# A diffusion layer's prologue: x by token halves, with squares, sums, power, rows and the first products by halves

## The chip, the cores and the metric

The kernel runs on one core of a Trainium2 chip. The core has a matrix engine (TensorE, PE in the profile, with its weight loads listed apart as PEld), three engines for elementwise work (VectorE or DVE, ScalarE or ACT, GpSimd or POOL), an engine that mainly issues transfers (SyncE or SP), and 16 DMA engines that carry the transfers between HBM and the on-chip memory SBUF. TensorE writes into PSUM, an accumulation memory of eight banks. The metric is the time of one execution on the device in microseconds (us), and the median over runs is compared.

## The reference

One layer over 512 latent tokens and 256 context tokens, each 1024 wide, in fp32. Only the start of it is touched by the change:

```python
def _rmsnorm(x, gain):
    xf = x.astype(jnp.float32)
    y = xf * lax.rsqrt(jnp.mean(xf * xf, axis=-1, keepdims=True) + EPS)
    return y.astype(x.dtype) * gain

def _modulate(x, gain, shift, scale):
    return _rmsnorm(x, gain) * (1 + scale) + shift

mod = jax.nn.silu(c) @ w_ada[l] + b_ada[l]
mod_c = jax.nn.silu(c_ctx) @ w_ada[l] + b_ada[l]
sh1, sc1, g1, sh2, sc2, g2 = jnp.split(mod[:, None, :], 6, axis=-1)
csh1, csc1, cg1, csh2, csc2, cg2 = jnp.split(mod_c, 6)
a_lat = _modulate(x, norm_mix[l], sh1, sc1)
a_ctx = _modulate(xc, norm_mix[l], csh1, csc1)
p_lat = jnp.split(a_lat @ w_in, split_at, axis=-1)
```

So for each token the squares of its 1024 values are summed and turned into a reciprocal root; x is multiplied by it and by a scale per channel, a shift per channel is added, and the result goes into the input projection. Scale and shift come from a product of silu(c) with a weight matrix of 1024 x 6144. Behind it follow pooling branches, a bidirectional mLSTM, an output projection, a second norm, a SwiGLU FFN and a final norm, which the change leaves as they are.

## The kernel before

Activations lie transposed: channels on the 128 partitions, tokens along the row. The 1024 channels are eight tiles of 128, numbered k, and x is eight tiles of 128x512. fp32 products are made of two rounded parts, high and low, of both operands: three matmuls (high by high, high by low, low by high) stand for one. A tile `a` of the modulated input therefore has a high part (ScalarE, line 300) and a low part (VectorE, line 303), and a weight block has `wh` (ScalarE, line 339) and `wl` (VectorE, line 341).

The prologue goes like this. `parm` (norm gains, biases, c) is fetched first on SP's queue (line 104), then x in four transfers of 512 KB (line 132), the identity matrix (line 137), and then, in turns, modulation weights `ada` of 1 MB for a tile k (line 275) and the first input-projection weights `wr` of 384 KB (line 338). `keep_warm` (line 143) issues filler matmuls of a zeroed 128x128 tile, whose result nobody reads; `WARM` (line 46) holds five counts of them.

ScalarE squares seven of the eight x tiles (line 355), VectorE squares the eighth (line 358) and adds them up into two tiles (lines 357, 359). TensorE sums these two over the partitions with the square tile as the stationary operand and two columns of ones as the moving one: four token blocks of 128, two tiles, so eight matmuls (line 362). `power` brings the sums to the power of -0.5 (VectorE line 243, GpSimd line 245), and `rstd_rows` spreads the result over the partitions with four matmuls against the identity (line 253).

`mod_rows(k)` multiplies silu(c) by the modulation weights with eight matmuls on quarter columns of the array (line 279), and ScalarE copies the 128x256 result (line 282). `mod_cols(k)` turns it by two transposes (line 288); VectorE adds the four quarters (line 290) and makes shift and scale (lines 292, 293). `stage(k)` fetches the weights, and makes `wh`, `wl` and the two parts of the tile `a` (lines 339, 299, 300, 341, 303). `products(k, lo, hi, parts)` then adds tile k into the six accumulators of 128x512 of the first six column blocks (line 347). In the steady state one step of the loop over k has 18 product matmuls, one `mod_rows`, one `mod_cols` and one `stage`, two tiles ahead. At k = 4 the context's column sums (line 237) and at k = 5 its rows (line 253) come in.

The order of the work around the change is written by hand: inside the manual schedule TensorE, ScalarE and VectorE run their instructions in the order of the code, and each engine waits in that order for its operands. SP issues its transfers in order too; a tile's buffer must be free before the transfer into it is issued (three buffers for `ada`, three for `wr`, two for `wh` and `wl`).

Of the kernel before, what the change touches and what calls it, by code (L numbers as in the profile page):

```python
# [10 lines left out]
F32 = mybir.dt.float32  # L11
F32R = mybir.dt.float32r
AF = mybir.ActivationFunctionType
ALU = mybir.AluOpType
# [3 lines left out]
P = 128  # L18
D = 1024
KT = D // P  # L20
T = 512
TC = 256
# [10 lines left out]
LINE = 256  # L33
HALFLINE = 64
NEXT = 48
WMAX = KT // 2 * (DH + NG)
# [14 lines left out]
def layer_kernel(ctx: ExitStack, tc, xT, cT, w0, w1, wv0, wv, wada_a, wada_b, par, crow, bg, wpool,  # L51
                 wout, wffi, wffo, icnt, consts, out):
    nc = tc.nc
    V = nc.vector
# [30 lines left out]
    open_pool("main", ("wr", "wh", "wl", "tmp", "small", "rc", "rc2"))  # L85
# [5 lines left out]
    def small(shape, nm, dtype=F32, home="small"):  # L91
        return homes[home].tile(shape, dtype, name=nm, tag=nm, bufs=1)
# [20 lines left out]
    warm = small([P, P], "warm", home="x")  # L113
# [6 lines left out]
    bsc1 = small([P, KT], "bsc1")  # L120
# [5 lines left out]
    quarter_mg = small([P, KT], "quarter_mg")  # L126
    V.tensor_scalar(quarter_mg, parm[:, C_MG:C_MG + KT], 0.25, None, ALU.mult)

    x_sb = []
    for k in range(0, KT, 2):  # L130
        xx = tl("x", [P, 2 * T], F32, KT // 2)
        nc.sync.dma_start(xx, xT[:, k * T:(k + 2) * T])
        x_sb += [xx[:, :T], xx[:, T:]]
    ones = small([P, P], "ones")
    nc.gpsimd.memset(ones, 1.0)
    ident = small([P, P], "ident")
    nc.sync.dma_start(ident, consts[:, :P])

    wbank = PS("pat")

    def keep_warm(n, zero):
        for i in range(n):
            nc.tensor.matmul(wbank[:, :zero.shape[-1]], zero, zero, start=True, stop=True)
# [60 lines left out]
    class SumSq:  # L204


        q = None
# [48 lines left out]
        free = False  # L256
        banks = []

    ALL = slice(0, T)
    HALF = (slice(0, T // 2), slice(T // 2, T))  # L260
# [11 lines left out]
    def mod_rows(k):  # L272

        raw = tl("ada", [P, KT, 256], F32, 3)
        nc.sync.dma_start(raw.rearrange("p k c -> p (k c)"), wada_a[k])
        acc = PS()
        for r in range(2):
            for g in range(4):
                nc.tensor.matmul(acc[32 * g:32 * g + 32, :256], sil[:, 4 * r + g, :], raw[:, 4 * r + g, :],
                                 start=r == 0, stop=r == 1, tile_position=(0, 32 * g))  # L280
        rows = S("tmp")
        nc.scalar.copy(rows[:, :256], acc[:, :256])
        return rows

    def mod_cols(k, rows):
        bank = PS()
        for w in range(2):
            nc.tensor.transpose(bank[:, w * P:(w + 1) * P], rows[:, w * P:(w + 1) * P], ident)
        both = tl("rc2", [P, 2, 2], F32, 2)
        V.tensor_reduce(both, bank[:, :2 * P].rearrange("p (w g j) -> p w j g", w=2, g=4)[:, :, 0:2, :],  # L290
                        mybir.AxisListType.X, ALU.add)
        V.tensor_scalar(shm[:, k, :], both[:, 0, :], pcol(C_BA, k), None, ALU.add)
        V.tensor_scalar(sm[:, k, :], both[:, 1, :], bsc1[:, k:k + 1], pcol(C_NM, k), ALU.add, ALU.mult)

    def modulate(src, r, scale, shift, h, l, between=None):

# [9 lines left out]
    aT, acT = [], []  # L306
# [3 lines left out]
    stc = SumSq()  # L310
# [21 lines left out]
    w_first = []  # L332
# [11 lines left out]
    def products(k, lo, hi, parts=((0, 0), (0, 1), (1, 0))):  # L344
        for i in range(lo, hi):
            for w, x in parts:
                nc.tensor.matmul(acc0[i], w_first[k][i][w], aT[k][x], start=k + w + x == 0, stop=k == KT - 1 and w == 1)  # L347

    nf = len(FIRST)


    bank = PS()
    sq = [S("tmp") for _ in range(KT)]
    for k in range(KT - 1):
        nc.scalar.activation(sq[k], x_sb[k], AF.Square)
        if 0 < k < KT - 2:
            V.tensor_add(sq[0], sq[0], sq[k])
    V.tensor_mul(sq[KT - 1], x_sb[KT - 1], x_sb[KT - 1])
    V.tensor_add(sq[KT - 1], sq[KT - 2], sq[KT - 1])
    for t, q in enumerate((sq[0], sq[KT - 1])):  # L360
        for i in range(T // P):
            nc.tensor.matmul(bank[:, 2 * i:2 * i + 2], q[:, i * P:(i + 1) * P], ones[:, 0:2], start=t + i == 0,
                             stop=t == 1, skip_group_check=True)
        if t == 0:
            keep_warm(WARM[1], warm)
    sd = stx.power(bank, T // P)
    rows = mod_rows(0)
    keep_warm(WARM[2], warm)
    mod_cols(0, rows)
    r = stx.rstd_rows(sd, ALL)  # L370
    stage(0, r)
    keep_warm(WARM[3], warm)
    rows = mod_rows(1)
    keep_warm(WARM[4], warm)
    products(0, 0, nf, ((0, 0),))
    mod_cols(1, rows)
    nc.scalar.copy(rs_x, r)
    stage(1, rs_x)
    for k in range(KT):
        parts = ((0, 0), (0, 1), (1, 0))[0 if k else 1:]  # L380
        products(k, 0, nf // 2, parts)
        if k + 2 < KT:
            rows = mod_rows(k + 2)
        products(k, nf // 2, nf, parts)
        if k + 2 < KT:
            mod_cols(k + 2, rows)
            stage(k + 2, rs_x)
        if k < 4:
            nc.sync.dma_start(cxt[k], cT[:, k * 512:(k + 1) * 512])
            for e in range(2):  # L390
                stc.add(c_sb[2 * k + e], slice(0, TC))
# [620 lines left out]
    parts = {}  # L1012
# [397 lines left out]
```

## Time and profile before

| | us |
|---|---|
| median of 3 runs | 885.37 (885.31 to 886.13) |
| the profiled execution's own time | 886.11 |
| its span in the profile | 884.3 |
| TensorE busy in the span | 874.4 (99%) |
| VectorE, ScalarE, GpSimd busy | 614.7, 436.7, 66.7 |
| start of the first product matmul (line 347) | 18.12 |
| granted TensorE clock | 0.998 |

The span is the time from the first to the last instruction in the profile; the execution's own time is 1.8 us longer. The profile's chain of waits follows the work that ended last back through what released each piece; its first column is the start in us, the second the duration, then the engine, the tile and the line, and xN counts the hardware's instructions that are merged in the row. One fp32 matmul of a 128-column stationary tile shows as two such instructions: the 32 filler matmuls of the start stand as x64. Matmul ends are modelled, so starts are the safer numbers.

### The profile page before, as it was taken

To read this page: it belongs to the slowest core of one execution; us is meant where nothing else is said; L and a number is where in the kernel's file an instruction comes from. 1 tells how busy PE (TensorE), PEld (TensorE's weight loads), DVE (VectorE), ACT (ScalarE), POOL (GpSimd) and SP (SyncE) were. 2 spreads that over 40 slices of the span, in tenths; PEclk is the share of its full clock that TensorE was granted. 3 is DMA by queue.
4 is the path that set the end of the run, shared out by engine and by line. 5 is a ranking of instruction groups with operands and counts; after the bars stand their busy time and mean duration, and the time that the engine had idled before them with its cause. 6 is when DMAs were issued, how large, how long until landed. Compare 5 with 4: busy or idle time off the path is not lost.

```text
span 884.3 us, 15057 instructions
## 1 busy us (share of the span) xinstructions
PE 874.4 (99%) x5920; PEld 797.7 (90%) x5920; DVE 614.7 (70%) x1187; ACT 436.7 (49%) x823; POOL 66.7 (8%) x93
## 2 busy tenths in 40 slices
PE   9999999999999999999999999999999999999997
PEld 7689798899888998889988899999889998899996
DVE  4678677877876787767886767795366753867644
ACT  4464354455344453444455446673255741666542
POOL 0000010020000100000000000120011100111000
PEclk9999999999999999999999999999999999999999
DMA  9863021436252542434454830384366643755502
GB/s 349 324 196 113 25 72 57 164 113 180 72 187 88 170 141 84 155 109 135 142 149 125 294 111 1 104 221 107 95 176 147 145 119 87 206 142 125 144 1 96
DMA packets 41446, 120.88 MB, mean 137 GB/s; under 512 B 4480, under 2 KB 8864, under 8 KB 40352
## 3 DMA queue, kind: packets, MB, share of 16 engines
q1 hardware_dynamic: 35904, 109.96, 38.2%
q0 software_dynamic: 5472, 9.96, 6.8%
q8 instruction: 46, 0.75, 0.3%
q14 instruction: 24, 0.20, 0.1%
HBM read 116.22 MB, written 3.69 MB: 136 GB/s over the span
## 4 chain that ended last, share of the span: by engine, by line
PE 96%; DVE 1%; ACT 1%; DMA 1%; issue 0%; DVEq 0%; SPq 0%; ACTq 0%
PE ps L187 14%; PE ps L189 13%; PE ps L188 13%; PE ps L197 8%; PE ps L195 8%; PE ps L194 8%; PE pat L347 3%; PE ps L578 3%; PE ps L579 3%; PE ps L580 3%; PE pat L187 2%; PE pat L189 2%; PE pat L188 2%; PE pat L792 2%; PE pat L793 2%; PE pat L794 2%
## 5 line engine op out<-in xcount | busy, mean ns | idle before, releaser
L157 ACT CAST wh<-wr 128x1024 fp32r<-128x1024 f32 (+3 forms) x78 | 78.9, 1011 | 102.7 <-PE ps L188 45.6
L158 DVE TENSOR_TENSOR wl<-wr,wh 128x1024 fp32r<-128x1024 f32 (+3 forms) x78 | 92.6, 1188 | 35.9 <-ACT wh L157 23.8
L194 PE MATMUL ps<-a,wh 128*128 128x512 f32 x272 | 106.5, 392 | 0.0
L195 PE MATMUL ps<-a,wh 128*128 128x512 f32 x272 | 106.3, 391 | 0.0
L187 PE MATMUL ps<-act,wh 128*128 128x512 f32 (+1 forms) x199 | 69.2, 348 | 0.0
L188 PE MATMUL ps<-act,wh 128*128 128x512 f32 (+1 forms) x199 | 69.0, 347 | 0.0
L189 PE MATMUL ps<-act,wl 128*128 128x512 f32 (+1 forms) x199 | 69.0, 347 | 0.0
L197 PE MATMUL ps<-a,wl 128*128 128x512 f32 x272 | 68.0, 390 | 0.0
L195 PEld LDWEIGHTS ps<-a,wh 128*128 128x128 f32 x272 | 51.1, 188 | 10.2
L194 PEld LDWEIGHTS ps<-a,wh 128*128 128x128 f32 x272 | 51.1, 188 | 10.2
L197 PEld LDWEIGHTS ps<-a,wl 128*128 128x128 f32 x272 | 50.8, 188 | 10.5
L1030 POOL DMA_DIRECT2D ol<-in_wffi x38 | 33.4, 897 | 254.7 <-ACT ol L1029 124.4
L187 PE MATMUL ps<-hp,gh 128*128 128x256 f32 x176 | 49.9, 284 | 0.4 <-ACT gh L176 0.4
L189 PE MATMUL ps<-hp,ol 128*128 128x256 f32 x176 | 48.8, 277 | 0.5 <-DVE ol L1027 0.5
L188 PE MATMUL ps<-hp,gh 128*128 128x256 f32 x176 | 49.0, 278 | 0.0
L1251 DVE SCALAR_TENSOR_TENSOR x<-ps,lb,x 128x512 f32<-128x512 f32 (+1 forms) x32 | 19.6, 616 | 42.1 <-PE ps L189 42.1
L189 PE MATMUL ps<-hp,gl 128*128 128x256 f32 x176 | 48.9, 278 | 0.0
L187 PE MATMUL ps<-hp,oh 128*128 128x256 f32 x176 | 48.8, 277 | 0.0
L188 PE MATMUL ps<-hp,oh 128*128 128x256 f32 x176 | 48.7, 277 | 0.0
L537 DVE SCALAR_TENSOR_TENSOR pb<-pb,crow_s 128x1024 f32<-128x1024 f32 x32 | 38.9, 1233 | 10.1 <-DMA pb<-in_wada_b 10.1
L187 PEld LDWEIGHTS ps<-act,wh 128*128 128x128 f32 x199 | 37.5, 188 | 4.8
L188 PEld LDWEIGHTS ps<-act,wh 128*128 128x128 f32 x199 | 37.5, 188 | 4.8
(365 smaller groups left out, 2726.4 us busy)
## 6 DMA issues: line engine op xcount, KB each, us to landing
wr<-in_w SPq DMA_DIRECT2D x42, 512.0 KB, 3.5
pb<-in_wada_b SPq DMA_DIRECT2D x32, 512.0 KB, 4.2
wr<-in_wffi SPq DMA_DIRECT2D x25, 512.0 KB, 4.3
ur<-in_wffi SPq DMA_DIRECT2D x19, 512.0 KB, 4.0
ol<-in_wffi POOLq DMA_DIRECT2D x38, 256.0 KB, 4.9
ada<-in_wada_a SPq DMA_DIRECT2D x8, 1024.0 KB, 9.8
wr<-in_wffo SPq DMA_DIRECT2D x16, 448.0 KB, 3.6
wr<-in_wout SPq DMA_DIRECT2D x8, 512.0 KB, 3.5
```

What stands on the lines that cost most here:

```text
L157: nc.scalar.copy(wh, raw[:, :n])
L158: V.tensor_sub(wl, raw[:, :n], wh.bitcast(F32))
L187: nc.tensor.matmul(dst, wh, ah, start=first and i == 0, stop=False, skip_group_check=on)
L188: nc.tensor.matmul(dst, wh, al, start=False, stop=False, skip_group_check=on)
L189: nc.tensor.matmul(dst, wl, ah, start=False, stop=last and i == n - 1, skip_group_check=on)
L194: nc.tensor.matmul(dst, wh, ah, start=first and i == 0, stop=False)
L195: nc.tensor.matmul(dst, wh, al, start=False, stop=False)
L197: nc.tensor.matmul(dst, wl, ah, start=False, stop=last and i == len(wparts) - 1)
L347: nc.tensor.matmul(acc0[i], w_first[k][i][w], aT[k][x], start=k + w + x == 0, stop=k == KT - 1 and w == 1)
L537: V.scalar_tensor_tensor(wa[:, :D], wa[:, :D], 0.5, crow_s, ALU.mult, ALU.mult, accum_out=mods[:, i:i + 1])
L578: nc.tensor.matmul(acc[:, :n], ah, wh, start=kk == 0, stop=False)
L1030: nc.gpsimd.dma_start(l, dram, accum_op=ALU.add)
```

## The change

The change is confined to the prologue. It does seven things.

- The transfers: `parm` and the first token halves of x tiles 4 to 7 are issued on ScalarE's queue, the first halves of tiles 0 to 3 on SP's. x arrives in eight transfers of 256 KB (a pair of tiles by 256 tokens, rows of 1 KB). On SP's queue the identity, the first modulation weights (in two transfers of 512 KB) and then the four second halves follow.
- The squares: for each half, and each pair of tiles, one square tile is made (ScalarE for pairs 0 and 2, VectorE for pair 1, both for pair 3). They are no longer added on VectorE: TensorE sums each of them over the partitions, four matmuls for a pair, 16 for a half, 32 in all.
- Power and rows run by halves, on two token blocks each; the first half's rows stand in the middle of `mod_rows(0)`.
- `mod_cols` has two ordinary matmuls against a 128x2 tile `pick` instead of two transposes and VectorE's reduction, for all eight k. The result has two columns per matmul.
- The first tile's 18 products are done by halves: 36 matmuls with 256 moving columns.
- `mod_rows(2)` stands behind all products of k = 0, and `mod_cols(2)` and `stage(2)` in the middle of k = 1.
- The filler counts: 18 at the start, and 2, 0, 2, 4 behind the pairs of the first half, 2 inside `mod_rows(0)`, 4 behind it, and 2, 0, 2, 2 behind the pairs of the second half; 38 before and 38 now.

```diff
-WARM = (32, 2, 2, 2, 0)
+WARM = (18, (2, 0, 2, 4), 2, 4, (2, 0, 2, 2))
-    nc.sync.dma_start(parm, par)
+    nc.scalar.dma_start(parm, par)
-    x_sb = []
-    for k in range(0, KT, 2):
-        xx = tl("x", [P, 2 * T], F32, KT // 2)
-        nc.sync.dma_start(xx, xT[:, k * T:(k + 2) * T])
-        x_sb += [xx[:, :T], xx[:, T:]]
+    def x_load(queue, j, c):
+        queue.dma_start(halves(pair[j])[:, :, c], halves(xT[:, 2 * j * T:(2 * j + 2) * T])[:, :, c])
+    for j in range(KT // 2):
+        x_load(nc.scalar if j >= KT // 4 else nc.sync, j, HALF[0])
...
     nc.sync.dma_start(ident, consts[:, :P])
+    ada0 = tl("ada", [P, KT, 256], F32, 3)
+    for r in range(2):
+        nc.sync.dma_start(ada0[:, 4 * r:4 * r + 4, :].rearrange("p k c -> p (k c)"),
+                          wada_a[0][:, 4 * r * 256:(4 * r + 4) * 256])
+    for j in range(KT // 2):
+        x_load(nc.sync, j, HALF[1])
...
     def mod_cols(k, rows):
         bank = PS()
-        for w in range(2):
-            nc.tensor.transpose(bank[:, w * P:(w + 1) * P], rows[:, w * P:(w + 1) * P], ident)
-        both = tl("rc2", [P, 2, 2], F32, 2)
-        V.tensor_reduce(both, bank[:, :2 * P].rearrange("p (w g j) -> p w j g", w=2, g=4)[:, :, 0:2, :],
-                        mybir.AxisListType.X, ALU.add)
+        for w in (1, 0):
+            nc.tensor.matmul(bank[:, 2 * w:2 * w + 2], rows[:, w * P:(w + 1) * P], pick, start=True, stop=True)
...
-    for t, q in enumerate((sq[0], sq[KT - 1])):
-        for i in range(T // P):
-            nc.tensor.matmul(bank[:, 2 * i:2 * i + 2], q[:, i * P:(i + 1) * P], ones[:, 0:2], start=t + i == 0,
-                             stop=t == 1, skip_group_check=True)
+    def column_sums(h, j, sq):
+        for e in range(2):
+            for i in range(2):
+                nc.tensor.matmul(sums[h][:, 2 * i:2 * i + 2], sq[:, (2 * e + i) * P:(2 * e + i + 1) * P], ones[:, 0:2],
+                                 start=j + e + i == 0, stop=j + e == KT // 2, skip_group_check=True)
...
+    for j in range(KT // 2):
+        sq = squares(0, j)
+        column_sums(0, j, sq)
+        keep_warm(WARM[1][j], warm)
+    sd = stx.power(sums[0], 2)
...
+    rows = mod_rows(0, lambda: (rs.append(rows_of(sd)), keep_warm(WARM[2], warm)))
+    keep_warm(WARM[3], warm)
+    sq2 = [squares(1, j) for j in range(2)]
     mod_cols(0, rows)
...
+    sq2 += [squares(1, j) for j in range(2, KT // 2)]
+    for j in range(KT // 2):
+        column_sums(1, j, sq2[j])
+        keep_warm(WARM[4][j], warm)
+    sd = stx.power(sums[1], 2)
...
+    products(0, 0, nf, ((0, 0),), HALF[0])
+    rs.append(rows_of(sd))
...
+    products(0, 0, nf, ((0, 1),), HALF[0])
+    products(0, 0, nf, ((1, 0),), HALF[0])
+    rows = mod_rows(1)
+    products(0, 0, nf, ((0, 0),), HALF[1])
+    products(0, 0, nf // 2, ((0, 1),), HALF[1])
     mod_cols(1, rows)
...
```

What stands on an engine's queue is shown by its own list of instructions (the names are tiles with a running number; x4 counts equal rows). TensorE before, from its start to the first product of k = 0; line 143 is the filler, 362 the column sums, 279 `mod_rows`, 288 `mod_cols`, 253 the rows, 347 a product:

```order
L143 MATMUL pat_109<-warm 128x128 x32
L362 MATMUL ps_158<-ones,tmp_159 128x2 x4
L143 MATMUL pat_109<-warm 128x128 x2
L362 MATMUL ps_158<-ones,tmp_166 128x2 x4
L279 MATMUL ps_196<-ada_194,sil 32x256 x8
L143 MATMUL pat_109<-warm 128x128 x2
L288 MATMUL ps_209<-ident,tmp_205 128x128 x2
L253 MATMUL ps_216<-ident,rc_191 128x128 x4
L143 MATMUL pat_109<-warm 128x128 x2
L279 MATMUL ps_237<-ada_235,sil 32x256 x8
L347 MATMUL ps_148<-a_226,wh_222 128x512
```

Eight column sums stand ahead of the first product, and both `mod_rows(0)` and `mod_rows(1)`.

TensorE of the changed kernel, the first part of the same stretch; line 157 is now the filler, 383 the column sums, 295 `mod_rows`, 389 the rows:

```order
L157 MATMUL pat_116<-warm 128x128 x18
L383 MATMUL pat_146<-ones,tmp_152 128x2 x4
L157 MATMUL pat_116<-warm 128x128 x2
L383 MATMUL pat_146<-ones,tmp_160 128x2 x4
L383 MATMUL pat_146<-ones,tmp_166 128x2 x4
L157 MATMUL pat_116<-warm 128x128 x2
L383 MATMUL pat_146<-ones,tmp_174 128x2 x4
L157 MATMUL pat_116<-warm 128x128 x4
L295 MATMUL ps_189<-ada_109,sil 32x256 x4
L389 MATMUL ps_194<-ident,rc_185 128x128 x2
L157 MATMUL pat_116<-warm 128x128 x2
L295 MATMUL ps_189<-ada_109,sil 32x256 x4
```

The first half's 16 column sums stand ahead of `mod_rows(0)`, which is cut in two by the rows of that half. The rest of the stretch follows at once; line 304 is the new `mod_cols`, 360 a product:

```order
L157 MATMUL pat_116<-warm 128x128 x4
L304 MATMUL ps_213<-pick,tmp_203 128x2 x2
L383 MATMUL pat_145<-ones,tmp_209 128x2 x4
L157 MATMUL pat_116<-warm 128x128 x2
L383 MATMUL pat_145<-ones,tmp_211 128x2 x4
L383 MATMUL pat_145<-ones,tmp_226 128x2 x4
L157 MATMUL pat_116<-warm 128x128 x2
L383 MATMUL pat_145<-ones,tmp_228 128x2 x4
L157 MATMUL pat_116<-warm 128x128 x2
L360 MATMUL ps_142<-a_223,wh_219 128x256
```

The second half's 16 column sums stand ahead of the first product, and `mod_rows(1)` has moved behind the first half's 18 products.

More of the change, by code (lines that the diff above doesn't have):

```diff
@@ L270, in layer_kernel, with mod_rows @@
     shm = small([P, KT, 2], "shm")
-    def mod_rows(k):
-        raw = tl("ada", [P, KT, 256], F32, 3)
-        nc.sync.dma_start(raw.rearrange("p k c -> p (k c)"), wada_a[k])
+    pick = small([P, 2], "pick")
+    def mod_rows(k, between=None):
+        if k == 0:
+            raw = ada0
+        else:
+            raw = tl("ada", [P, KT, 256], F32, 3)
+            nc.sync.dma_start(raw.rearrange("p k c -> p (k c)"), wada_a[k])
         acc = PS()
         for r in range(2):
+            if r and between:
+                between()
             for g in range(4):
@@ L342, in stage, with products @@
         w_first.append([(wh[:, i * P:(i + 1) * P], wl[:, i * P:(i + 1) * P]) for i in range(len(FIRST))])
-    def products(k, lo, hi, parts=((0, 0), (0, 1), (1, 0))):
+    def products(k, lo, hi, parts=((0, 0), (0, 1), (1, 0)), c=ALL):
         for i in range(lo, hi):
             for w, x in parts:
-                nc.tensor.matmul(acc0[i], w_first[k][i][w], aT[k][x], start=k + w + x == 0, stop=k == KT - 1 and w == 1)
+                nc.tensor.matmul(acc0[i][:, c], w_first[k][i][w], aT[k][x][:, c],
+                                 start=k + w + x + c.start == 0, stop=k == KT - 1 and w == 1, skip_group_check=True)
@@ L366, in layer_kernel, with squares @@
-    sd = stx.power(bank, T // P)
-    rows = mod_rows(0)
-    keep_warm(WARM[2], warm)
-    mod_cols(0, rows)
-    r = stx.rstd_rows(sd, ALL)
-    stage(0, r)
-    keep_warm(WARM[3], warm)
+    sums = [acc0[4 - h] for h in range(2)]
+    def squares(h, j):
+        sq = S("tmp")
+        src, dst = halves(pair[j])[:, :, HALF[h]], halves(sq)
+        if j == KT // 2 - 1:
+            nc.scalar.activation(dst[:, 0], src[:, 0], AF.Square)
+            V.tensor_mul(dst[:, 1], src[:, 1], src[:, 1])
+        elif j % 2:
+            V.tensor_mul(dst, src, src)
+        else:
+            nc.scalar.activation(dst, src, AF.Square)
+        return sq
@@ new lines, in column_sums, with rows_of @@
+    def column_sums(h, j, sq):
[3 more added lines that the diff above has]
+                                 start=j + e + i == 0, stop=j + e == KT // 2, skip_group_check=True)
+    def rows_of(sd):
+        r = PS()
+        for i in range(2):
+            nc.tensor.matmul(r[:, i * P:(i + 1) * P], sd[:, i:i + 1].broadcast_to([P, P]), ident, start=True, stop=True)
+        return r[:, :T // 2]
@@ new lines, in layer_kernel @@
+    nc.sync.dma_start(raw[:, :n], w0[0])
+    t0, a0h, a0l = S("tmp"), S("a", F32R), S("a", F32R)
+    aT.append((a0h, a0l))
+    w_first.append([(wh[:, i * P:(i + 1) * P], wl[:, i * P:(i + 1) * P]) for i in range(nf)])
+    V.scalar_tensor_tensor(t0[:, HALF[0]], x_sb[0][:, HALF[0]], sm[:, 0, 0:1], rs[0], ALU.mult, ALU.mult)
+    sq2 += [squares(1, j) for j in range(2, KT // 2)]
[3 more added lines that the diff above has]
+    sd = stx.power(sums[1], 2)
@@ new lines, in layer_kernel @@
+    nc.scalar.activation(a0h[:, HALF[0]], t0[:, HALF[0]], AF.Identity, bias=shm[:, 0, 0:1])
+    V.scalar_tensor_tensor(a0l[:, HALF[0]], t0[:, HALF[0]], shm[:, 0, 0:1], a0h[:, HALF[0]].bitcast(F32),
+                           ALU.add, ALU.subtract)
+    for c in (slice(0, n // 2), slice(n // 2, n)):
+        nc.scalar.copy(wh[:, c], raw[:, c])
+        V.tensor_sub(wl[:, c], raw[:, c], wh[:, c].bitcast(F32))
+    nc.scalar.copy(rs_x[:, HALF[0]], rs[0])
+    products(0, 0, nf, ((0, 0),), HALF[0])
@@ L373, in layer_kernel, with context_squares @@
     rows = mod_rows(1)
-    keep_warm(WARM[4], warm)
-    products(0, 0, nf, ((0, 0),))
+    products(0, 0, nf, ((0, 0),), HALF[1])
+    products(0, 0, nf // 2, ((0, 1),), HALF[1])
     mod_cols(1, rows)
-    nc.scalar.copy(rs_x, r)
     stage(1, rs_x)
-    for k in range(KT):
-        parts = ((0, 0), (0, 1), (1, 0))[0 if k else 1:]
-        products(k, 0, nf // 2, parts)
+    products(0, nf // 2, nf, ((0, 1),), HALF[1])
+    products(0, 0, nf, ((1, 0),), HALF[1])
+    rows = mod_rows(2)
+    def context_squares(k):
+        nc.sync.dma_start(cxt[k], cT[:, k * 512:(k + 1) * 512])
+        for e in range(2):
+            stc.add(c_sb[2 * k + e], slice(0, TC))
@@ L382, in layer_kernel @@
+    for k in range(1, KT):
+        products(k, 0, nf // 2)
+        if k == 1:
+            mod_cols(2, rows)
+            stage(2, rs_x)
+            context_squares(0)
         if k + 2 < KT:
             rows = mod_rows(k + 2)
-        products(k, nf // 2, nf, parts)
+        products(k, nf // 2, nf)
         if k + 2 < KT:
@@ L388, in layer_kernel @@
         if k < 4:
-            nc.sync.dma_start(cxt[k], cT[:, k * 512:(k + 1) * 512])
-            for e in range(2):
-                stc.add(c_sb[2 * k + e], slice(0, TC))
+            context_squares(k)
         if k == 4:
```

33 lines of the change are left out of this document (18 added, 15 removed).

## The prediction

> **What bounds the kernel now.** I read the page's busy times first, then the chain of waits, then the first 60 us of that chain in order of time, where the change lies.
>
> ```profile
> PE 874.4 (99%) x5920; PEld 797.7 (90%) x5920; DVE 614.7 (70%) x1187; ACT 436.7 (49%) x823; POOL 66.7 (8%) x93
> PE 96%; DVE 1%; ACT 1%; DMA 1%; issue 0%; DVEq 0%; SPq 0%; ACTq 0%
> ```
>
> The first row is busy time by engine, the second the chain's shares. TensorE carries 96% of the chain, so what is added to its queue should reach the end, and what is taken from another engine's should not. Whether that also holds in the prologue is read from the chain there (start, duration, engine, line; two hardware instructions to one fp32 matmul):
>
> ```profile
> 1.36 9.85 PE pat L143 x64
> 11.21 0.12 issue
> 11.33 1.02 PE ps L362 x8
> 12.36 0.55 PE pat L143 x4
> 12.91 0.79 PE ps L362 x8
> 13.70 1.00 PE ps L279 x16
> ...
> 15.63 0.91 PE ps L253 x8
> 16.56 0.76 DVE tmp L299
> 18.12 0.73 PE ps L347 x2
> 19.77 0.22 PE ps L288 x2
> ...
> 22.38 1.59 PE pat L347 x6
> 23.97 0.22 PE ps L288 x2
> 24.19 1.38 PE ps L347 x6
> ...
> 37.43 1.00 PE ps L279 x16
> ...
> 43.01 1.00 PE ps L279 x16
> ...
> 46.52 0.34 PE ps L237 x4
> ...
> 49.04 1.00 PE ps L279 x16
> ```
>
> From 1.36 us on TensorE hardly pauses: 0.12 us before the first column sums, and even where the chain leaves it (16.54 to 18.12, the only place here) its own list shows it at work:
>
> ```profile
> 16.36 0.61 PE L143 MATMUL pat<-warm 128*128 128x128 f32 x4
> 16.90 1.07 PE L279 MATMUL ps<-ada,sil 128*32 128x256 f32 x16
> ```
>
> Fillers and `mod_rows(1)` cover that gap but for about 0.15 us. Much of what runs before 18.12 is filler, but it stands in an in-order queue, and the change keeps 38 of 38 fillers. So the prologue's time is the sum of what stands in TensorE's queue, fillers included, as long as nothing on it waits longer than now. That is the reading I predict from.
>
> **The column sums.** Eight matmuls become 32. Each has a new 128x128 stationary tile and two moving columns, so the two columns cannot be what it costs. The weight loads of the second group before:
>
> ```profile
> 12.64 0.97 PEld L362 LDWEIGHTS ps<-ones,tmp 128*128 128x128 f32 x8
> 13.63 0.59 PEld L279 LDWEIGHTS ps<-ada,sil 128*32 128x32 f32 x16
> L362 PEld LDWEIGHTS ps<-ones,tmp 128*128 128x128 f32 x16 | 1.9, 191 | 0.3 <-issue 0.3
> ```
>
> From 12.64 to 13.63 eight loads follow one another, 0.124 us each with the joint behind them; without the last one's own length (0.97 less 0.19, the mean of the third row, over seven) 0.111. I take 0.111, so 0.222 us for a matmul. Added: 24 x 0.222 = 5.3 us. Bounds are the two rows of the chain, 0.79 and 1.02 us for four matmuls: 24 x 0.198 = 4.7 and 24 x 0.255 = 6.1. VectorE's five additions and one more (lines 357, 359) go away; they hid behind fillers until 11.21 us, so they give nothing back.
>
> **The two matmuls of `mod_cols`.** The new form (128x128 stationary, two columns, fp32) is line 237's, which occurs once: a step of the loop, from one `mod_rows` to the next, takes 43.01 - 37.43 = 5.58 us, and with that pair in it 49.04 - 43.01 = 6.03. The pair costs 0.45 us; two transposes cost 0.22 (the row at 23.97). Difference 0.23. The pair's own row gives 0.34 and thus 0.12. I take 0.21, near the step's difference because that contains the joints: eight times, 1.7 us, bounds 1.0 and 1.9. The reduction taken from VectorE (line 290) lies beside TensorE's products.
>
> **The first tile by halves.** 18 matmuls of 512 columns become 36 of 256. Start-to-start of 256-column matmuls and the time of twelve 512-column ones:
>
> ```profile
> 561.29 0.12 PE pat L189
> 561.41 0.12 PE pat L187
> ...
> 58.48 2.72 PE pat L347 x12
> ```
>
> 36 x 0.12 = 4.32 against 18 x 0.227 = 4.08: 0.2 us more, bounds 0.1 and 0.5 (one more change between fp32 and rounded operands, 0.1, and 0.12 being rounded). The rows are four matmuls before and after, as `mod_rows(0)` has its eight.
>
> **What is waited for.** With these numbers TensorE's queue ahead of the first product is as follows. 18 fillers run to about 7.9 us: the rate of the fillers changes on the way,
>
> ```profile
> 2.16 1.28 PE pat L143 x6
> 8.20 1.12 PE pat L143 x10
> ```
>
> 0.213 us for one record in the first row, 0.112 in the second, with the change near 6.3 us: 24 slow and 12 fast records. Then 32 column sums (7.1), 20 fillers (4.5), `mod_rows(0)` (1.0), one half's rows (0.45) and `mod_cols(0)` (0.45): 13.5 us, so the first product starts near 21.4 instead of 18.12, and `mod_rows(1)`, done by then before, is still to come. Are the operands there? By bytes: 84 KB of `parm` and 2 MB of x went ahead of the identity and the first weights, and the landings were
>
> ```profile
> 1.19 1.84 SPq L132 DMA_DIRECT2D x<-in_xT  x4
> DMA to landing us min/median/max: 4.9/6.1/7.3
> 3.83 0.56 SPq L275 DMA_DIRECT2D ada<-in_wada_a  x1
> ada<-in_wada_a SPq DMA_DIRECT2D x1, 1024.0 KB, 9.4
> 4.43 0.44 SPq L338 DMA_DIRECT2D wr<-in_w  x1
> wr<-in_w SPq DMA_DIRECT2D x1, 384.0 KB, 9.8
> ```
>
> issue plus time to landing: x from 6.1 to 9.9 us, `ada` 13.2, the first `wr` 14.2. The change has the same bytes ahead of `wr`, and within them the order halves, identity, `ada`, halves: about 7.4 us for the last first half (the 1.1 MB that landed second before), 10.2 for `ada`, 13.2 for the last second half. TensorE reaches that last half's sums only near 20 us, so nothing there waits for a transfer, even at 2 us later. ScalarE issues three transfers ahead of its first work, 0.46 us each by SP's row, so silu(c) is ready some 1.4 us later than before, and `mod_rows(0)` wants it only near 13; SP issues the four second halves ahead of the first `wr`, and that lands by its place in the bytes, some 7 us before TensorE needs it. Behind the second half's sums (21.0 us) stand VectorE's line 257 and, queued behind it in order, the low part of `a` and `wl`; GpSimd's power is
>
> ```profile
> L245 POOL TENSOR_TENSOR rc<-rc,mhalf x6: 695/706/1146, 14.0 to 876.5; 128x2 f32<-128x2 f32 x5, 128x4 f32<-128x4 f32 x1
> 20.03 0.17 DVE L290 TENSOR_REDUCE rc<-ps 128x4 f32<-128x16 f32 x1 [1.18 <-PE ps L288]
> 22.31 0.75 DVE L303 SCALAR_TENSOR_TENSOR a<-tmp,shm,a 128x512 fp32r<-128x512 f32 x1
> ```
>
> 0.70 us on two columns, so the rows' operand is there at 22.1, just when the six products of the first half have run (21.4 + 0.7): no wait. One wait is new. The low part of tile 1 ended at 23.06 before, 3.07 us behind the end of `mod_cols(1)` (19.99), hence 2.9 without the reduction. Behind `mod_cols(1)` the queue now has nine half products (1.1), `mod_rows(2)` (1.0), the joint behind it (six products took 1.59 us at 22.38 and 1.38 at 24.19, so 0.2) and tile 1's first matmul (0.23): 2.5. I add 0.4 us, bounds 0 and 0.6.
>
> **The sum.** 5.3 + 1.7 + 0.2 + 0.4 = 7.6 us, less 0.1 for pauses before 18.12 that the fuller queue closes: **+7.5 us**. Bounds 4.7 + 1.0 + 0.1 + 0 = 5.8 and 6.1 + 1.9 + 0.5 + 0.6 = 9.1. The profiled execution took 886.11 us (span 884.3), so 893.6 by its own time; it lies 0.7 above the median of 885.37, against which I forecast **892.9 us**, 891.2 to 894.5 by the bounds. Later stages have TensorE on the chain for nearly all of the span and the same order, so I let the whole of it through.
>
> **Rivals.** *The transfers and the elementwise chain set the start, not the queue.* For it speaks that the old prologue's first 18 us contain over 10 us of filler. Then the first product would start when the first `wr` is there (14.2) and half of it rounded,
>
> ```profile
> 15.03 0.84 ACT L339 CAST wh<-wr 128x768 fp32r<-128x768 f32 x1
> ```
>
> half of 0.84 later, near 14.65 us, and TensorE would go on with 36 half products (4.3), rows (0.5), `mod_rows(1)` and `mod_rows(2)` with joints (2.4), `mod_cols(1)` (0.45) and the wait (0.4): tile 1 at 22.7, where before, `mod_cols(2)` started at 23.97. Of these 1.3 us the six later `mod_cols` take 6 x 0.21 = 1.3 back: 885.4, no change; with their price at 0.12 it would be faster by 0.6. The point from which it decides: fewer than about 13.3 us of work in the queue before the first product. By the rows there are 20, so it needs column sums that cost next to nothing. The mechanism could be weight loads that run under the fillers; against it, each filler loads weights of its own.
>
> *TensorE's clock falls back.* The fillers' two rates above are a factor of 1.9 apart, while the profile's granted clock is 0.998 over the whole span, so this state isn't seen there. Between 7.9 and 21.4 us most of what the queue holds streams two columns; only 20 fillers, the rows and `mod_rows(0)` stream more. The slow stretch at the start lasted from 1.36 to about 6.3 us and held 24 records where 44 would fit, a loss of 20 x 0.112 = 2.2 us. Two such stretches: 4.5 us more, 897.4. Against it: between 11.33 and 16.54 column sums, fillers and rows alternated at the fast rate. The Trainium skill (TensorE: Matmul & The Clock Gate, Part 1: The HAM clock gate) says that the array's clock is halved by default, released after a window of about 3.4 us of activity and halved again after an idle one; this trace agrees on the first change and shows no second one, and by that rule the question is whether two-column matmuls count as activity.
>
> *Part of the added loads is hidden.* If half of each column sum ran under its neighbours, 2.7 us would go and 890.2 be left; the two rows of the chain speak against it, since four matmuls with work on both sides cost 0.79 and 1.02.
>
> **Chances and range.** Forecast 0.74, hidden loads 0.07, clock 0.07, the transfers' chain 0.12. The first three are slower; the last I split into 0.08 within and 0.04 faster. About 0.2% (1.8 us) is what a measurement can tell from no change. The range 889.3 to 896 takes in the forecast's bounds, the hidden loads and the beginning of the clock's case.
>
> **What would show it.** Right: the first product at 21 to 22 us; the weight loads of line 383 at 0.11 us each without pauses; no wait of TensorE on a square or a transfer between 8 and 21 us; a step of the loop near 5.8 us instead of 5.58; the distance to before growing from some 6 us at k = 1 to 7.5 at the end of k = 7 and constant from there. Wrong: loads of line 383 shorter than 0.1; TensorE idle before the first product at 15 to 16 us (the transfers' chain); records of line 157 or 383 at 0.2 us behind 8 us (the clock); a difference at 61 us that is gone by the end.

## The result and the profile after

The changed kernel takes 897.27 us (median of 4 runs, 896.82 to 898.77) beside 885.65 us before (4 runs, 885.31 to 886.13): 1.0132 of before, 95% interval 1.0120 to 1.0144, so 11.6 us slower. The forecast was 892.9 with a range up to 896.0. The direction was right and the size was not. The profiled execution took 896.82 us with a span of 895.0.

The page of the changed kernel, busy times by engine and the chain's shares:

```profile
PE 885.8 (99%) x6002; PEld 810.0 (91%) x6002; DVE 611.1 (68%) x1181; ACT 436.1 (49%) x825; POOL 67.0 (7%) x94
PE 98%; DVE 1%; ACT 1%; issue 0%; DVEq 0%
```

TensorE is busy for 11.4 us more, the span is 10.7 us longer, and TensorE's share of the chain rose from 96 to 98%: what was added stands in TensorE's queue, as forecast. The chain of the changed kernel in order of time (start, duration, engine, line; line 157 is the filler, 383 the column sums, 295 `mod_rows`, 389 the rows, 360 a product):

```profile
7.61 0.79 PE pat L383 x8
8.40 0.55 PE pat L157 x4
8.95 1.68 PE pat L383 x16
...
11.97 1.47 PE pat L157 x8
13.44 1.01 PE ps L295 x8
14.45 1.16 PE ps L389 x4
15.60 0.57 PE pat L157 x4
16.18 0.57 PE ps L295 x8
16.74 1.09 PE pat L157 x8
...
22.64 1.01 PE pat L157 x4
23.65 0.43 PE ps L360 x2
...
41.02 1.00 PE ps L295 x16
...
46.83 1.00 PE ps L295 x16
```

The first product starts at 23.65 instead of 18.12; 21.4 was forecast. Two things in these rows do not fit a queue at one rate. The same eight records of line 295 take 1.01 us at 13.44 and 0.57 at 16.18, and four filler records take 0.55 us at 8.40 and 1.01 at 22.64. The changed kernel by stretches of 1 us (length, TensorE's busy time and records, granted clock, share of the transfer engines, GB/s):

```profile
12.00:13.00 1.00, 1.00 (x7) 0.67 1.09 400
13.00:14.00 1.00, 1.00 (x11) 0.50 1.09 443
14.00:15.00 1.00, 1.00 (x11) 0.50 1.00 418
15.00:16.00 1.00, 1.00 (x7) 0.63 0.95 375
...
22.00:23.00 1.00, 1.00 (x8) 0.79 0.96 394
23.00:24.00 1.00, 1.00 (x7) 0.50 0.21 82
24.00:25.00 1.00, 1.00 (x7) 0.50 0.06 25
25.00:26.00 1.00, 1.00 (x6) 0.51 0.59 150
```

TensorE's clock falls to half twice, while the engine is busy all the time. Read as full and half clock only, the first stretch holds 0.66 + 1 + 1 + 0.74 = 3.4 us at half, the second 0.42 + 1 + 1 + 0.98 = 3.4. They begin at 12.34 and 22.58, 10.2 us apart. In the windows between them (16 to 22 us) the clock is at 1.00. Before, all windows of 4 us from 4 to 32 us stand at 1.00, as this one:

```profile
12.00:16.00 4.00, 4.00 (x43) 1.00 1.03 429
```

The distance to before is 9.40 us at the fourth step of the loop (46.83 against 37.43) and grows by 0.2 a step. At the end of k = 7 it is 10.06 us (71.26 against 61.20). It then holds, near 9.4 to 10, up to 840 us, and grows again in the last FFN block, from 9.5 to 11.0. That block in before, 26 us of it, with the columns as above:

```profile
846.00:872.00 26.00, 26.00 (x231) 1.00 0.01 4
```

and the same stretch of the changed kernel, 10 us later:

```profile
856.00:882.00 26.00, 26.00 (x222) 1.00 0.01 2
```

Without any wait and at a clock of 1.00, TensorE gets through 222 matmuls instead of 231. Nothing in the diff touches this block. So three things make up the 11.6 us: work in the prologue, the clock, and something at the far end. The experiments take them apart. The experiments ran in four groups of four, each with runs of before on the same chip; before's median was 885.3 to 885.9 us in them, so kernels of different groups are compared by their ratios to before.

### The profile page after: what moved, and what is told of

The parts are those of the page before. It is cut to its first block, busy times and chain, and to the rows that moved or that the text cites. A ratio compares the mean times of both kernels' runs of the same rounds, so it can differ in the third digit from the quotient of the medians.

```text
span 895.0 us, 15228 instructions
## 1 busy us (share of the span) xinstructions
PE 885.8 (99%) x6002; PEld 810.0 (91%) x6002; DVE 611.1 (68%) x1181; ACT 436.1 (49%) x825; POOL 67.0 (7%) x94
## 4 chain that ended last, share of the span: by engine, by line
PE 98%; DVE 1%; ACT 1%; issue 0%; DVEq 0%
PE ps L201 14%; PE ps L202 13%; PE ps L203 13%; PE ps L211 8%; PE ps L209 8%; PE ps L208 8%; PE ps L645 3%; PE ps L647 3%; PE ps L646 3%; PE pat L360 3%; PE pat L201 2%; PE pat L202 2%; PE pat L203 2%; PE pat L859 2%; PE pat L860 2%; PE pat L861 2%
## 5 line engine op out<-in xcount | busy, mean ns | idle before, releaser
L209 PEld LDWEIGHTS ps<-a,wh 128*128 128x128 f32 x272 | 51.1, 188 | 10.2
L604 DVE SCALAR_TENSOR_TENSOR pb<-pb,crow_s 128x1024 f32<-128x1024 f32 x32 | 39.2, 1242 | 11.3 <-DMA pb<-in_wada_b 11.2
```

Of the source, the lines that this page charges most:

```text
L209: nc.tensor.matmul(dst, wh, al, start=False, stop=False)
L604: V.scalar_tensor_tensor(wa[:, :D], wa[:, :D], 0.5, crow_s, ALU.mult, ALU.mult, accum_out=mods[:, i:i + 1])
```

## The experiments on the clock

The theory after the result: column sums with two moving columns keep the weight loads busy but not the array, and when most of a few microseconds consists of them, the clock falls. Rivals: the fall comes from the stretch being long, whatever streams; or it comes from the transfers.

### Column sums that stream 128 columns

```diff
-nc.tensor.matmul(sums[h][:, 2 * i:2 * i + 2], sq[...], ones[:, 0:2], ...)
+nc.tensor.matmul(sums[h][:, P * i:P * i + P], sq[...], ones, ...)
```

> The changed kernel with each of the 32 column sums streaming 128 columns of ones instead of 2; the number of matmuls and weight loads is the same. Theory A (TensorE's clock falls to half where the queue streams few columns; two stretches from about 12 and 22.5 us cost some 3 us): granted clock 1.00 between 12 and 28 us, first product near 22 instead of 23.65 us, time 894.3 (893.8 to 895). Rival W (the excess over the forecast of 892.9 is waits for GpSimd's power, 1.14 and 0.87 us there, and for the low part of tile 1): first product stays at 23.6, time 897.3 or a little more.

Measured: 894.67 us against 885.30 (1.0104, interval 1.0089 to 1.0119). The same stretches of this kernel in windows of 4 us:

```profile
12.00:16.00 4.00, 3.99 (x40) 1.00 1.05 407
20.00:24.00 4.00, 3.96 (x35) 1.00 0.95 371
24.00:28.00 4.00, 4.00 (x43) 1.00 0.76 237
```

The clock stays at 1.00 and the first product starts at 21.72 instead of 23.65, although the wide sums are the dearer ones. The granted clock over the whole span is 0.998 to 0.999 in all four executions, against 0.995 in all four of the changed kernel. The number of matmuls, their stationary tiles and the transfers are the same; only the columns that stream differ. So the two-column sums are the cause of the fall, and not the length of the stretch or the transfers by themselves.

### The later fillers left out

```diff
-WARM = (18, (2, 0, 2, 4), 2, 4, (2, 0, 2, 2))
+WARM = (18, (0, 0, 0, 0), 0, 0, (0, 0, 0, 0))
```

> The changed kernel with only the 18 fillers at the start; the 20 later ones, which take 6.3 us in its profile, are gone. If the clock fell no further: 897.3 - 6.3 = 891.0, first product near 17.4 us. Theory A: without them hardly anything streams, the clock falls earlier and stays low until products have run for some 3 us: first product at 18 to 20 us, granted clock near 0.5 over more than 6 us in sum, time 892 to 895.

Measured: 896.90 us (1.0128, interval 1.0111 to 1.0145). In the chain of this kernel the 16 column sums of the second half follow one another,

```profile
16.34 6.83 PE pat L383 x32
23.16 0.64 PE ps L360 x2
```

and by windows of 4 us

```profile
12.00:16.00 4.00, 3.05 (x20) 0.56 1.04 410
16.00:20.00 4.00, 4.00 (x20) 0.50 1.02 406
20.00:24.00 4.00, 4.00 (x19) 0.50 0.85 343
```

Twenty fillers less, and the first product starts only 0.5 us earlier. One part of that is a transfer: the first half's last sums began at 10.51, behind a square that waited for x until 10.0, where the changed kernel was through with them at 11.97. The larger part is the clock. 32 records in 6.83 us are 0.213 each, twice what they cost in the changed kernel (0.79 for eight). So the fillers were not only ballast: without them the clock does not come back between the two halves.

### The kernel before with 32 column sums

```diff
-        if 0 < k < KT - 2:
-            V.tensor_add(sq[0], sq[0], sq[k])
...
-    for t, q in enumerate((sq[0], sq[KT - 1])):
+    for t, q in enumerate(sq):
```

> The kernel before with VectorE's six additions of square tiles left out and all eight square tiles summed by TensorE, 32 column sums in one run instead of 8 in two; nothing else is changed. Theory S (the queue's sum, 24 x 0.207 us by the changed kernel's rows): 5.0 us more than before, 890.4. Theory A on top: 28 column sums in a row stream two columns each for some 6 us, so the granted clock falls to 0.5 for at least one stretch behind 13 us, 1.5 to 3 us more: 892 to 893.5. Rival H (part of the sums is hidden): 888 to 889.

Measured: 896.17 us against 885.29 (1.0127, interval 1.0110 to 1.0145), some 3 us more than expected. The chain and the windows of this kernel:

```profile
10.23 7.57 PE ps L359 x56
...
20.36 1.86 PE ps L279 x16
```

```profile
12.00:16.00 4.00, 4.00 (x33) 0.84 1.04 427
16.00:20.00 4.00, 4.00 (x20) 0.50 0.95 388
20.00:24.00 4.00, 4.00 (x26) 0.50 0.24 52
```

28 sums in a row go along with a clock at half for some 10 us (1.3 + 4 + 4 us by these windows, and 1 behind); `mod_rows(0)` behind them takes 1.86 us instead of 1.00. One part of the change alone costs the kernel before nearly all that the whole change cost. The expectation had taken the changed kernel's two short falls as the measure, where fillers stand between the sums.

### Pairs added on VectorE, 16 column sums

```diff
+        V.tensor_add(term, term, sq)
+        column_sums(0, j, term)
```

> The changed kernel with the square tiles of two pairs added on VectorE ahead of the column sums: 16 column sums instead of 32, four additions of 128x512 more on VectorE, fillers as they are. Theory S: 16 x 0.21 = 3.3 us less, 894.0; with theory A the sparse stretches are half as long, and where the clock then stays up another 1.5 to 3 us go: 891 to 892.5. Rival W (waits on the elementwise engines set the start): the additions lengthen that chain by 0.7 us each, 897 or more.

A miss: 898.37 us (894.72 to 901.22; 1.0143, interval 1.0115 to 1.0172), and the profiled execution is the slowest of the four. With half the sums gone, the last pair's first half of x had no cover. The chain of this kernel starts with that transfer, and its second window of 4 us is nearly empty:

```profile
1.74 9.22 DMA x<-in_xT
```

```profile
8.00:12.00 4.00, 1.28 (x11) 1.00 1.05 379
12.00:16.00 4.00, 3.74 (x20) 0.63 1.02 403
```

Here TensorE idles for 2.7 of 4 us and then runs at half clock. So a fall also came behind an idle stretch, with two-column sums next to it; which of the two brought it is not separated here. The fastest execution, 894.72, had a granted clock of 0.997 over the span where the others had 0.993 to 0.994, so the spread goes with the clock, and this run says nothing on the price of the sums.

## The experiments on `mod_cols` and on the end of the kernel

### The old and the new `mod_cols`, each in the other kernel

The changed kernel with the two transposes and the reduction of before:

```diff
-            nc.tensor.matmul(bank[:, 2 * w:2 * w + 2], rows[:, w * P:(w + 1) * P], pick, start=True, stop=True)
+            nc.tensor.transpose(bank[:, w * P:(w + 1) * P], rows[:, w * P:(w + 1) * P], ident)
+        both = tl("rc2", [P, 2, 2], F32, 2)
+        V.tensor_reduce(both, ...)
```

> The changed kernel with mod_cols as before (two transposes, VectorE's reduction). Theory S (the sum over TensorE's queue, 0.235 us for each of eight): 895.4, a step of the loop back at 5.58 us from 5.82; both stretches of half clock stay. Rival P (the pair costs only its own row's 0.12 more): 896.3.

Measured: 893.92 us (1.0097, interval 1.0082 to 1.0112), 3.1 us below the changed kernel by the ratios, where 1.9 were expected. The loop's step in the chain of this kernel, from the third to the fourth, is 46.05 - 40.46 = 5.59 us, where the changed kernel has 5.81:

```profile
40.46 1.00 PE ps L294 x16
...
46.05 1.00 PE ps L294 x16
```

The kernel before with the new `mod_cols`, the same edit the other way round:

> The kernel before with mod_cols as in the change (two matmuls with two columns instead of two transposes and VectorE's reduction), nothing else. By the steps of the changed kernel's chain, 5.81 against 5.58 us: 8 x 0.235 = 1.9 us more than before, 887.2; clock 1.00 as before. By the difference of the rows alone (0.34 against 0.22): 1.0 more, 886.3. If it is worth what undoing it gave in the changed kernel (3.3 us): 888.6.

Measured: 889.97 us against 885.29 (1.0054, interval 1.0037 to 1.0071): 4.7 us for a step whose work can be worth 2. Matched row by row with before, TensorE is 1.8 us late at 62 us, 2.3 at 437 us, and 3.9 at the end; 1.5 us of that arise behind 837 us. Both misses point to the block at the end. What the new `mod_cols` does to it is to move memory: two 32-byte buffers of the reduction's result go and the 32-byte place of `pick` comes, so that some thirty kinds of tiles behind them lie 32 bytes lower (those aligned to 256 bytes keep their place or move by a whole line). `act`, the moving operand of the last FFN block, is aligned to 64 bytes there and starts 128 bytes behind a multiple of 256 instead of 192. The new `mod_cols` is in the changed kernel and in the wide sums too, the old one in before.

### Wide sums and transposes together

Both edits above in the changed kernel.

> The changed kernel with both: column sums that stream 128 columns, and mod_cols as before. Clock 1.00 throughout, so what is left is the queue's sum: 894.7 (wide sums alone) less 1.9 = 892.8, which is 7.4 above before, and of that 5.3 column sums. If undoing mod_cols is worth the 3.3 us that it gave in the changed kernel: 891.3.

Measured: 891.74 us (1.0073, interval 1.0058 to 1.0088). It is taken up again below, since its end contradicted the reading just given.

### Only the places

The changed kernel, the kernel before, and two of the experiments, each with the same instructions in the same order on every engine, and tiles moved. First the changed kernel with one unused tile, so that the tiles behind it lie at their old places (but for the tile kinds `ada` and `cx`, which the change lets swap places, by multiples of 256 bytes):

```diff
-    pick = small([P, 2], "pick")
+    pick, _ = small([P, 2], "pick"), tl("rc2", [P, 8], F32)
```

> The changed kernel with one unused 32-byte tile beside pick, so that every tile behind it lies at its old place in SBUF (the change takes two 32-byte buffers away and adds one, so all behind lay 32 bytes lower, and the last FFN block's moving operands 64 bytes lower); every engine's instructions and their order are the same. Theory P (the places set the rate of the last block, 0.1187 us a matmul of 256 columns against 0.1133 over the last 40 us, at a granted clock of 1.00 in both): the last block returns to 0.1133, the distance to before stops growing behind 840 us (it grew from 9.6 to 10.94 us there), and the time is 1.3 us below the changed kernel, 896.0. Rival (the rate belongs to the single execution, since the wide-sums kernel with transposes has the old places and yet 0.1178): no change, 897.3.

Measured: 895.35 us against 885.84 (1.0112, interval 1.0097 to 1.0128). Its last block:

```profile
856.00:882.00 26.00, 26.00 (x231) 1.00 0.05 16
```

Then the kernel before with one buffer for the reduction's result, so that all behind it lies 32 bytes lower:

```diff
-        both = tl("rc2", [P, 2, 2], F32, 2)
+        both = tl("rc2", [P, 2, 2], F32, 1)
```

> The kernel before with one buffer for the reduction's result in mod_cols instead of two, so that all tiles behind it lie 32 bytes lower, as in the changed kernel; writer and reader are both VectorE, in order, so nothing waits. Theory P: the last block runs at 0.1187 us a matmul and the time is 1.3 to 1.6 us above before, 886.6 to 886.9. Rival: no change, 885.3.

Measured: 887.62 us (1.0021, interval 1.0012 to 1.0029). Its last block:

```profile
846.00:872.00 26.00, 26.00 (x222) 1.00 0.01 1
```

Both come out as the theory of the places says, a little stronger: 1.8 us less and 1.8 us more. The kernel before with the new `mod_cols`, and the same unused tile for the old places:

> The kernel before with the new mod_cols, which took 889.97 against 885.29 with 1.9 us of the 4.7 in the prologue, and the old places restored by an unused tile. Theory P: the growth behind 840 us (2.5 to 3.9) goes, and perhaps the 0.5 us between 222 and 461 us: 888.0 to 888.6, that is 885.3 plus the prologue's 1.9 and 0.6 to 1. Rival: no change, 890.

Measured: 888.14 us (1.0029, interval 1.0018 to 1.0040). So the new `mod_cols` costs 2.3 us and not 4.7. And the changed kernel with wide sums and the old places, that is, without the clock's fall and without the shift:

> The changed kernel with column sums that stream 128 columns (894.67, the clock at 1.00 throughout) and the old places restored. Theory P and the clock theory together: 894.67 less 1.3 to 1.6, 893.2 (893.0 to 893.4), of which 7.2 us stand in the prologue, near the forecast's sum of 7.5. If the places do nothing: 894.7.

Measured: 892.98 us (1.0082, interval 1.0068 to 1.0096). Three rows of its chain:

```profile
21.93 0.24 PE ps L360 x2
...
38.46 1.00 PE ps L295 x16
...
44.26 1.00 PE ps L295 x16
```

The first product starts at 21.93, inside the forecast's 21 to 22, and at the fourth step the distance to before is 44.26 - 37.43 = 6.8 us; at the end of k = 7 it is 7.4, and from there to the last matmul it stays between 7.1 and 8.1.

### Only the last block's operand

Which tiles' places count was open. The kernel before with `act` alone moved, to 128 bytes behind a multiple of 256:

```diff
-    tl("before_act", [P, NEXT], F32, 1, LINE)
+    tl("before_act", [P, NEXT], F32, 1, LINE), tl("pad", [P, 48], F32, 1, HALFLINE)
```

> The kernel before with an unused tile ahead of the last FFN block's operands act, so that only these move: their start modulo 256 bytes is 128 as in the changed kernel, instead of 192; no other tile and no instruction moves. If the place of this moving operand alone sets the rate: 222 matmuls in 26 us of the last block instead of 231, and 1.4 to 1.8 us above before, as with all tiles moved (887.62 against 885.84). If other tiles' places do it: no change.

Measured: 887.04 us against 885.87 (1.0013, interval 1.0004 to 1.0022).

```profile
846.00:872.00 26.00, 26.00 (x222) 1.00 0.00 1
```

The same with `act` at a multiple of 256 (a pad of 16 elements):

> The kernel before with act alone moved to a start of 0 modulo 256 bytes. If the start's remainder sets the rate of the last block, it is another than at 192: slower by up to 1.8 us (887.6) if 192 is the one good place, the same as before if only 128 is bad. If act's place is nothing: 885.8.

Measured: 887.82 us (1.0022, interval 1.0013 to 1.0031).

```profile
846.00:872.00 26.00, 26.00 (x220) 1.00 0.01 1
```

The changed kernel with `act` alone moved back to 192 (a pad of 64 elements):

> The changed kernel with an unused tile ahead of act, so that only act moves and starts at 192 modulo 256 bytes, as it did before the change. If the place of act alone does it: 231 matmuls in 26 us and 895.4 to 895.9, as with all old places. If not: 897.3.

Measured: 896.53 us (896.21 to 897.94; 1.0122, interval 1.0108 to 1.0136). The profiled execution is the slowest of the four, 897.94:

```profile
856.00:882.00 26.00, 26.00 (x224) 1.00 0.01 1
```

And the kernel with wide sums and transposes once more, whose first profiled execution (892.54, again the slowest of its four) had 224 matmuls in such a stretch at the old place:

> The kernel with wide sums and transposes once more, unchanged; act lies at 192 modulo 256. If its slow last block belonged to the one execution: 231 matmuls in 26 us now and a time near 1.0057 of before (its prologue's 5.6 us against 885.8 give 890.9 to 891.4). If it belongs to the kernel: 222 to 224 matmuls again and 1.0073 of before, 892.3.

Measured: 891.20 us (1.0062, interval 1.0046 to 1.0077).

```profile
851.00:877.00 26.00, 26.00 (x231) 1.00 0.01 2
```

So in the kernel before the operand's start alone changes the rate of the block: 231 in 26 us at 192, 222 at 128, 220 at 0, with no other difference in the program, and the medians follow, by 1.2 and 2.0 us. That 1.2 stands beside the 1.8 us of all moved tiles. The rest, if there is one (the intervals overlap), belongs to other tiles that moved; which, was not tried.

In the changed kernel it is not shown. The expected 231 did not come, and the 1.0122 against 1.0132 is no price for the operand, because the clock differed too: in the profiled execution it stood at half for 10.2 us of the prologue instead of 6.9, and the granted clock over the whole span was 0.992, 0.996, 0.993 and 0.993 in the four executions, where the changed kernel had 0.995 in each. Over all traces, eight of the ten with `act` at 192 have 231 and two have 224, and all seven with 128 have 222. The two with 224 are each the slowest execution of its kernel, and the one of these kernels that ran again then had 231; a single execution can thus be slow at the right place, and why stays open.

### An attempt at a version that beats before

The halves kept, with the ballast taken out: pairs added on VectorE where the squares are early (20 sums), wide sums, transposes, 25 fillers, all first halves on SP's queue.

```diff
-WARM = (18, (2, 0, 2, 4), 2, 4, (2, 0, 2, 2))
+WARM = (18, (2, 0, 3, 0), 0, 2, (0, 0, 0, 0))
-        x_load(nc.scalar if j >= KT // 4 else nc.sync, j, HALF[0])
+        x_load(nc.sync, j, HALF[0])
+        V.tensor_add(sq, sq, squares(0, j + 1))
+        column_sums(0, sq, j == 0, j > 0)
...
+    V.tensor_add(sq2[0], sq2[0], sq2[1])
```

> The halves with the queue thinned: pairs of square tiles added on VectorE (20 column sums instead of 32: 8 for the first half, 12 for the second), sums that stream 128 columns, mod_cols as before, all first halves of x on SP's queue, 25 fillers instead of 38. Theory S and A together: the first product at 16 to 17 us, the first tile's second step near 23.4 instead of 24.2 before, clock 1.00; time 884.5 to 886 beside 885.3 before. Rival W (VectorE's chain or late transfers set the start): TensorE idle for some us ahead of the first product, the clock falls behind that, 888 or more.

Measured: 888.15 us against 885.29 (1.0029, interval 1.0018 to 1.0040): still slower. The chain of this kernel has left TensorE at two places, for the second half's power and for tile 1's low part:

```profile
17.15 0.88 POOL rc L259
...
24.13 0.95 DVE wl L356
25.08 0.69 DVE a L318
25.77 0.04 issue
25.81 1.42 PE ps L362 x5
```

Tile 1's products start at 25.81 where before, `products(1)` stood at 24.19. With the queue emptied, the elementwise chains set these two places, the rival that the prediction named first. Of the kernels run, the kernel before remains the fastest.

## Why the prediction was right and wrong

**What bounds the kernel.** Right: TensorE's queue. No wait on a square or a transfer appears in the changed kernel between 8 and 21 us, as forecast.

**Column sums, 5.3.** The six groups in the changed kernel's chain add up to 6.62 us for 32, 0.207 each, so 24 cost 5.0. Inside the bounds. The sentence "so the two columns cannot be what it costs" was right on the price at full clock and hid their effect: two columns are what takes the clock down.

**`mod_cols`, 1.7.** The step is 46.83 - 41.02 = 5.81 us against 5.58: 0.23, so 1.9 over eight. As a whole, in pairs of kernels with the same places, the new form cost 2.3 us in the kernel before, 1.3 in the changed kernel (1.0112 against 1.0097), and 0.8 or 1.8 with wide sums (1.0082 against 1.0073 and, run again, 1.0062). Each ratio is uncertain by some 0.0015, so these agree with the rows. Right.

**First tile by halves, 0.2, and the wait for tile 1, 0.4.** Six half products take 0.24 + 0.47 us (21.93 in the run without the clock's fall), so 36 take 4.3, as forecast; TensorE's wait for tile 1's low part shows in the changed kernel's list of waits, 0.2 us and inside the bounds:

```profile
PE ps L360 <- DVE a L316: 0.2, 1, 0.2
```

**The sum, 7.5.** With the clock held and the places restored it is 892.98 - 885.84 = 7.1 us. The wide sums in that run are a little dearer: its six groups (0.89, 1.79, 0.89, 1.00, 1.79, 0.89) take 7.25 us, 0.6 more than 6.62, but the fillers right behind four of them show 0.45 instead of 0.55 each. From the first sum of a half to the end of its last, 0.1 us more remains (12.28 - 7.81 = 4.47 against 11.97 - 7.61 = 4.36), and the same in the second half. So the work by itself is about 6.9 us, inside 5.8 to 9.1. This part of the prediction held.

**The rival of the clock, chance 0.07: wrong to set it aside.** This is the step that failed first: the sum has no term for the clock, and the clock was no rival but an addition to the sum. The first fall, at 12.34, lies in the place that was named (between 7.9 and 21.4 us), the second begins behind it, at 22.58, at the end of the second half's sums. The sign that was named, fillers at 0.2 us a record, is there at 11.97 and 22.64. Two arguments led to it. The row held against the clock, column sums at the fast rate between 11.33 and 16.54 before, showed eight sums with other work between, and was carried over to 32. And the price, 2.2 us for a stretch, came from the start's longer stretch (1.36 to 6.3 us). The runs show 895.35 - 892.98 = 2.4 us for both falls together, and with the 0.2 us by which the wide sums hide it, 2.6. The rows give 3.0: from the eight fillers behind the first half's sums to `mod_rows(1)` the changed kernel takes 27.36 - 11.97 = 15.4 us and the kernel with wide sums and old places 24.82 - 12.28 = 12.5, with 0.1 of dearer sums in it. That the rival's 897.4 is nearly the measured time is luck: its 4.5 us were too dear by 1.5 to 1.9, and the places, which it did not have, make up for that.

The Trainium skill (TensorE: Matmul & The Clock Gate, Part 1: The HAM clock gate) states a free-running window of 3.4 us by which the clock follows the engine's activity. The traces agree on the window: both falls here last 3.4 us and begin three times 3.4 us apart, and the clock stays at half for 10.2 us behind 28 sums in a row and for some 13.6 us without the later fillers, about three and four times 3.4. What the prediction left open, whether two-column matmuls count as activity, the runs answer: a stretch made mostly of them let the clock fall though the profile shows the engine busy for all of it. That the profile's clock does not show this state held for the start alone; behind 8 us it does.

**"So I let the whole of it through": wrong by 1.8 us.** The distance is not constant from 61 us on. The step treated the program behind the prologue as the same because its instructions and order are the same. Their addresses are not: 1.8 us came from tiles that lie elsewhere, most of them 32 or 64 bytes lower. By the traces 1.5 of it arises in the last block (the distance grows there from 9.5 to 11.0, and not at all with the old places), and in the kernel before 1.2 came from one operand of that block.

**The whole.** 6.9 of work, 2.6 of clock and 1.8 of places are 11.3 of the 11.6 us measured; what is left lies within the runs' scatter. That this sum comes out proves nothing, since the three parts are the differences between the same four kernels, one after the other. What confirms them is measured apart from it: the clock's 3.0 by the rows, the places' 1.8 in the kernel before, and the prologue's 7.4 at the end of k = 7 without the falls.

**The other rivals.** Transfers as the bound: not so here, but the run with pairs added shows the case, with the queue thinned and one transfer landing late. Hidden loads: no, the sums cost 0.207 each, no less than before's faster row (0.198).

## What to carry to other kernels

Before adding many matmuls with few moving columns in one stretch, look at the granted clock by windows of a microsecond: with the engine 100% busy, the clock can still fall to half, and here streaming more columns, at nearly the same price, kept it up. Removing or adding a small tile moves every tile behind it, so in a kernel whose operands were placed by hand, compare addresses as well as the order of instructions, and read the distance between two traces up to the end, not only past the change. Take a stated rival with a mechanism and a place as a possible addition to the sum, and let the range hold both.

## What the runs showed of the hardware that was not expected

- The start of a moving operand modulo 256 bytes changes the rate of fp32 matmuls with 256 moving columns in one block of this kernel: 231 in 26 us at 192, 222 at 128, 220 at 0, nearly without transfers in that stretch. Why 192 is the best of the three, and what took it to 224 in two executions, is not shown.
- The same transfer lands at very different times. The first half of the last pair of x, third on ScalarE's queue in nine kernels with equal transfers, let its square on ScalarE start at 6.8 to 11.0 us; the transfer was issued at 1.7 us each time. With fillers and sums standing ahead, even 9.2 us (the kernel with wide sums) left no pause on TensorE between 8 and 12 us; with the sums halved, 11.0 us left one of 2.7.
- The granted clock of before reads 1.00 from 4 to 8 us, where fillers run at the slow rate up to 6.3; that of the kernel without the later fillers reads 0.50 where its sums run at the same rate, 0.213 us a record. So the column showed the falls in mid-kernel here and not the slow start.
